# A list scheduler's prices refitted, instruction chunks counted, and ranks moved by pseudo-random offsets, in one layer of RWKV-7, gated DeltaNet and SwiGLU

## The chip, the cores and the metric

The kernel runs on one core of a Trainium2 chip, in one launch. The metric is the device time of an execution in microseconds (us), as the median of several runs. Engines are named as in the profile: PE is TensorE (matmuls), DVE is VectorE, ACT is ScalarE, POOL is GpSimd, and SP is SyncE, whose queue issues most DMA transfers.

## The reference, cut to what matters

One layer over 256 latent and 256 context tokens of 2048 channels, in fp32. The modulated, normalised input goes through one wide projection. Its columns feed two token mixers, each run in both directions: an RWKV-7 scan of 16 heads of 64 channels, and a gated DeltaNet of 8 heads of 128 channels in chunks of 64 tokens. A chunk needs the solution of a unit lower triangular system, and the chunks of a head are tied together by a state:

```python
sol = lax.linalg.triangular_solve(lmat, rhs, left_side=True, lower=True, unit_diagonal=True)
...
def step(s, inp):
    qk_i, u_i, w_i, qd_i, kt_i, gl_i = inp
    v_new = u_i - jnp.einsum('bhck,bhkv->bhcv', w_i, s)
    o = jnp.einsum('bhck,bhkv->bhcv', qd_i, s) + jnp.einsum('bhcj,bhjv->bhcv', qk_i, v_new)
    s = s * gl_i[..., None, None] + jnp.einsum('bhck,bhcv->bhkv', kt_i, v_new)
    return s, o
...
m = jax.nn.sigmoid(g_a) * (o_a @ p_a) + jax.nn.sigmoid(g_b) * (o_b @ p_b)
return m @ w_out
...
return (jax.nn.silu(gate) * up) @ w_down
```

The mixers' outputs are projected, merged with sigmoid gates and projected once more; then the layer's feed-forward part follows. The silu, sigmoid, exponential, logarithm and tanh in it run on ACT, which holds one set of function tables at a time; an instruction ACT_TABLE_LOAD brings another set.

## The kernel before, in words

**Products.** Each large fp32 product is made of three products of a shorter format. A 128x128 block of weights is split into an upper half (tile whi, a cast on ACT) and a lower half (wlo, the difference, on DVE); the activations are split likewise (hxh and hxl for the latent tokens, hch and hcl for the context, ob for the DeltaNet's output). PE then adds whi times upper, whi times lower and wlo times upper in PSUM (tile mm), each as a row "mm" of 128x256. These rows are nine tenths of PE's work; they need only the weights, so they fit anywhere. The mixers' products are small, in full fp32, and pass through the PSUM tiles s, pa and pi: 128x128 for the scans of the DeltaNet heads (tiles St for the state, Rg, Qe, Vn, aw for the parts of a step), 32x32 blocks with 16 or 32 columns for the triangular inverses (tiles iv, LT, Qm, extra, Tx). An fp32 product of this kind counts once in the listing of the program's order, and as two passes in the trace. Between two small products of a head stands work of DVE or ACT nearly always.

**Stages.** The prologue (L495 to L595: the first modulation vectors and the low-rank columns) ends at 124.5 us. From there to 1337.7 us runs what I call the weave: input projection, both mixers, and most of the projections behind them. The last stage (rest of the merge, output projection, feed-forward; products L436 to L438, casts L426 and L427) follows to the end in a fixed order.

**The scheduler.** The order within the weave is chosen while the program is built, by the class Weave (from L218). Every task is a generator that yields operations, waits for names (`yield "asked", i, q`), or asks for a buffer. `Weave.add` takes one with a rank: the products of weights have rank 900, a pair p of RWKV heads has ranks about 10p, DeltaNet head h has 100 + 10h + i. `Weave.run` (L274) holds a model of the time at which each engine is free, and picks the piece that could start first; on equal starts the lower rank. A chosen operation is appended to its engine's instructions, and the engine's modelled time grows by its price: `Lane.product` (L119) for matmuls, `Lane.cost` for the others. `Weave.turn` adds for a change of PE's tile size (into a small one, back to full, across between two small ones), with the values of `LAT` at L31. Since all operations are issued by the lambda at L164, nearly every instruction of the weave has that line in the profile; a table load that a task asks for by itself has L154.

The chip executes each engine's instructions in just this order, and semaphores hold an engine where its operand isn't there. A price that differs from the chip changes no result, only the order.

**What is told of readiness.** Two names are given out by tasks when the last of several pieces of work is done. `lowrank_out` (four per RWKV pair, j from 0 to 3) tells "lowrank" when j is 3, and `gate_out` (40 in all) tells "gates" when j is 39.

Of the kernel before, what the change touches and what calls it, by code (L numbers as in the profile page):

```python
# [2 lines left out]

# [9 lines left out]
F32R = mybir.dt.float32r  # L13
# [5 lines left out]
P = 128  # L19
# [8 lines left out]
NHELD, NB = 6, 10  # L28
GATES_A, GATES_B = ((36,0,0,0,0,0,0,0),(0,0,0,0,0,4,0,0))

LAT = dict(dma=3.1, v=1.0, s=1.0, hop=dict(e=0.215, v=0.135, s=0.15, g=0.1), slack=0.1, own=0.09, grp=32, crank=-1, cg=4, into=0.14, back=0.2, cross=0.14, stay=0.0, gpace=1.6)  # L31
LNEXP = "natural_log_exp_and_others"
SIGM = "sigmoid_and_others"
UNIT = 64 * 64 + 64
# [71 lines left out]
class Op:  # L106


    def __init__(self, lane, cost, call, mode=None, base=None):
        self.lane, self.cost, self.call, self.mode, self.base = lane, cost, call, mode, base  # L110


class Lane:
# [5 lines left out]
    def product(self, out, a):  # L119
        n, rows, m = int(np.prod(out.shape[1:])), a[0].shape[0], int(np.prod(a[0].shape[1:]))  # L120
        if a[0].dtype == F32R and n == T:
            return 0.1145, "full"
        if a[0].dtype == F32R:
            return 0.0065 + 0.000443 * n, "full"
        if rows >= 96 and m == P:
            return max(0.219, 0.012 + n * 4 / 2400), "full"
        mode = (rows, m)
        if rows < 64:
            return 0.0165, mode
        if rows == 64:  # L130
            return (0.064 if n > 64 else 0.048) if m < P else 0.02 + n * 4 / 2400, mode
        return (0.06 if m < 64 else 0.058), mode

    def cost(self, name, out, a, k):
        n = int(np.prod(out.shape[1:]))
# [14 lines left out]
    def __getattr__(self, name):  # L150

        def op(out, *a, **k):
            if name == "preload_act_table_set":
                return Op(self, 1.2, lambda: self.engine.preload_act_table_set(out))  # L154
            if name == "dma_start":
                return Op(self, 0.6 if self.each > 0.002 else 0.06, lambda: self.engine.dma_start(out, *a))
            mode = base = None
            if name == "transpose" and len(a) == 2:
                cost, mode = 0.109, "full"
            elif name == "matmul":  # L160
                cost, mode = self.product(out, a)
            else:
                cost, base = self.cost(name, out, a, k), (out.offset // out.ap[0][0], out.shape[0])
            return Op(self, cost, lambda: getattr(self.engine, name)(out, *a, **k), mode, base)  # L164
        return op


# [50 lines left out]
class Weave:  # L218


    def __init__(self):
        self.work, self.free, self.done, self.now, self.mode, self.cur, self.idle = [], {}, {}, 0.0, "full", None, True

    def add(self, rank, gen, at=None):
        now, cur = self.now, self.cur
        w = Piece(rank, gen, now if at is None else at)
        self.work.append(w)
        self.step(w, None)
        self.now, self.cur = now, cur
# [37 lines left out]

    def release(self, banks):
        banks.free.append(self.cur.shown())

    def turn(self, mode):
        return 0.0 if mode == self.mode else LAT["back"] if mode == "full" else LAT["into"] if self.mode == "full" else LAT["cross"]

    def run(self):  # L274
        while self.work:
            for w in list(self.work):
                if w.want is not None and not isinstance(w.want, (list, float)) and self.there(w):
                    self.step(w, self.take(w))
            best = None
            for w in self.work:  # L280
                if isinstance(w.want, float):
                    key = (w.seen, w.rank)
                    if best is None or key < best[0]:
                        best = (key, w, None)
                elif isinstance(w.want, list):
                    lane = w.want[0].lane
                    start = max(self.free.get(lane, 0.0), w.at(lane))
                    if lane is self.tensor and self.mode != "full" and w.want[0].mode == "full":
                        start += LAT["stay"]
                    key = (start, w.rank)  # L290
                    if best is None or key < best[0]:
                        best = (key, w, lane)
            if best is None:
                if any(w.want is not None and not isinstance(w.want, (list, float)) and self.there(w) for w in self.work):
                    continue
                assert not self.work, [w.want for w in self.work]
                return
            w, lane = best[1:]
            if lane is None:
                w.want = None  # L300
                assert w.seen < 1e5, [x.want for x in self.work]
                self.step(w, None)
                continue
            start = max(self.free.get(lane, 0.0), w.at(lane))
            ops, rest = w.want, None
            cost = 0.0
            if lane is self.tensor:
                ops, rest = ops[:LAT['grp']], ops[LAT['grp']:]
                if self.mode == "full" and ops[0].mode == "full" and start > self.free.get(lane, 0.0) + 0.02:
                    cost += 0.1  # L310
            w.want = rest or None
            got = []
            for o in ops:
                if lane is self.tensor:
                    cost += self.turn(o.mode)
                    self.mode = o.mode
                elif o.base is not None:
                    if lane.base not in (None, o.base):
                        cost += 0.08
                    lane.base = o.base  # L320
                got.append(o.call())
                cost += o.cost
            w.end = self.free[lane] = start + cost
            w.lane = lane
            if not rest:
                self.step(w, got[-1])


def emit(ctx: ExitStack, tc, A, out, dbg=None):
# [473 lines left out]
    pr[0]["kps"], pr[0]["rps"] = low[4], low[5]  # L803
    sgd = rs.tile([P, T], F32, tag="sgd", name="sgd")[:64]

    def lowrank_out(p, j, ps, so):
        yield s.activation(so, ps, AF.Sigmoid, bias=p_("w0" if j < 2 else "a0", 8 * (j % 2) + p))
        weave.release(psb)
        yield s.dma_start(sgd_[p, :, j], so)
        yield 2.5  # L810
        if j == 3:
            weave.ready("lowrank", p)

    landed = {}
# [328 lines left out]


    gts_ = dpool.tile([40, P, T], F32, name="gts_")
    gate_next = iter(range(40))

    def gate_out(pool, j, ps):
        g = pool.tile([P, T], F32, tag="gt", name="gt")
        yield s.copy(g, ps[:, :T])  # L1150
        weave.release(mmb)
        Q.dma_start(gts_[j], g)
        if j == 39:
            weave.ready("gates")

    def fetch(parts, i):
# [234 lines left out]
    class Shared:  # L1391


        def __init__(self):
            self.arena, self.iv = Places(None, arena, *gplaces), []
# [476 lines left out]
    with tc.manual_schedule(engines={mybir.EngineType.PE, mybir.EngineType.DVE, mybir.EngineType.Activation,  # L1872
                                     mybir.EngineType.SP}):
        for j in range(NB, KT):
            ps = pst(pmm, "mm")
            block(ps[:, 0:T], (j - NB) * NGH // CG, range(NGH), OB)
            m = x1p.tile([P, T], F32, tag="m", name="m")
# [15 lines left out]
        for j in range(KT):  # L1893
# [7 lines left out]
            k, a = divmod(j, 4)  # L1901
# [190 lines left out]
```

## Time and profile before

| what | value |
|---|---|
| median of 3 runs | 2196.24 us (2191.26 to 2198.05) |
| span of the profiled execution | 2188.6 us |
| prologue | 0 to 124.5 us |
| weave | 124.5 to 1337.7 us |
| last stage | 1337.7 to 2188.6 us |
| PE, DVE, ACT busy | 96%, 71%, 51% |

The profiled execution is one execution, 7.6 us under the median of the runs. In the rows, "out<-in" names the tiles that an instruction writes and reads; a bracket at the end of a row of the timeline is the engine's idle time just before it with what ended that. "issue" there means that the engine waited for nothing that the profile shows. The granted PE clock is 1 at full speed.

### The profile page before, as it was taken

Reading aid. Unit: us, or ns where it says so; the run is one execution under the profiler, and the core shown is the slowest. Engines: PE = TensorE matmul, PEld = TensorE weight load, DVE = VectorE, ACT = ScalarE, POOL = GpSimd, SP = SyncE. Lnnn points to the kernel's source line nnn. Section 1 sums busy time; section 2 is a strip of 40 time slices with the busy share of each in tenths; the row PEclk is TensorE's granted clock in tenths of the full one; section 3 lists DMA queues with packets and bytes.
Section 4 is the critical chain, followed back from the end, with each engine's and each line's share of the span. In section 5 each row is a group of like instructions: output and inputs, shape, how many; then the busy total and the mean of one; then the engine's idle time right before and its main releaser. Section 6 shows DMA issues by size and latency. Waiting matters only on the chain.

```text
span 2188.6 us, 59116 instructions
## 1 busy us (share of the span) xinstructions
PE 2108.6 (96%) x24536; PEld 1977.7 (90%) x24536; DVE 1552.5 (71%) x3308; ACT 1118.2 (51%) x2209; POOL 19.2 (1%) x55
## 2 busy tenths in 40 slices
PE   7999999999999999999999998999999999999997
PEld 5897698889888888998989987999999999999997
DVE  4466589889889976899998776865666665555554
ACT  3246654565455556565565754644444444444443
POOL 0000000000000000000000000000000000000000
PEclk9999999999999999999999999999999999999999
DMA  9966756645555554665653754856777776666665
GB/s 377 415 175 196 228 154 179 178 144 156 154 167 143 166 164 135 188 194 171 176 152 112 216 153 157 297 177 201 238 248 235 242 241 217 194 191 194 195 194 163
DMA packets 276286, 431.14 MB, mean 197 GB/s; under 512 B 119857, under 2 KB 136625, under 8 KB 271665
## 3 DMA queue, kind: packets, MB, share of 16 engines
q1 hardware_dynamic: 262192, 402.19, 59.5%
q10 hardware_dynamic: 13824, 25.17, 3.6%
q8 instruction: 192, 3.15, 0.6%
q14 instruction: 78, 0.63, 0.1%
HBM read 401.50 MB, written 25.77 MB: 195 GB/s over the span
## 4 chain that ended last, share of the span: by engine, by line
PE 80%; DVE 7%; DMA 7%; ACT 3%; issue 2%; SPq 0%; DVEq 0%; ACTq 0%
PE mm L164 26%; PE mm L438 12%; PE mm L436 12%; PE mm L437 12%; PE s L164 6%; PE pa L164 5%; PE pi L164 3%; DVE arena L164 2%; DMA wraw<-w 2%; DVE wlo L164 2%; DMA wraw<-ada_rest 1%; PE mm L529 1%; PE s L579 1%; ACT arena L164 1%; PE mm L579 1%
## 5 line engine op out<-in xcount | busy, mean ns | idle before, releaser
L427 DVE TENSOR_TENSOR wlo<-wraw,whi 128x1024 fp32r<-128x1024 f32 (+1 forms) x264 | 314.9, 1193 | 291.0 <-ACT whi L426 291.0
L426 ACT CAST whi<-wraw 128x1024 fp32r<-128x1024 f32 (+1 forms) x264 | 270.6, 1025 | 386.1 <-PE mm L437 359.5
L164 PE MATMUL mm<-hxh,wlo 128*128 128x256 f32 x1376 | 399.9, 291 | 9.5 <-DVE wlo L164 7.7
L164 PE MATMUL mm<-hxh,whi 128*128 128x256 f32 x1376 | 397.0, 288 | 2.3 <-ACT whi L164 1.3
L164 PE MATMUL mm<-hxl,whi 128*128 128x256 f32 x1376 | 395.4, 287 | 0.0
L438 PE MATMUL mm<-hfh,wlo 128*128 128x256 f32 x1344 | 371.8, 277 | 0.2 <-DVE wlo L427 0.2
L436 PE MATMUL mm<-hfh,whi 128*128 128x256 f32 x1344 | 371.2, 276 | 0.0
L437 PE MATMUL mm<-hfl,whi 128*128 128x256 f32 x1344 | 371.2, 276 | 0.0
L164 ACT CAST whi<-wraw 128x512 fp32r<-128x512 f32 (+1 forms) x398 | 242.8, 616 | 214.9 <-PE mm L164 93.2
L164 DVE TENSOR_TENSOR wlo<-wraw,whi 128x512 fp32r<-128x512 f32 (+1 forms) x398 | 270.3, 682 | 86.2 <-ACT whi L164 79.8
L164 PEld LDWEIGHTS mm<-hxh,wlo 128*128 128x128 f32 x1376 | 260.7, 189 | 19.6 <-DVE wlo L164 11.3
L164 PEld LDWEIGHTS mm<-hxh,whi 128*128 128x128 f32 x1376 | 260.6, 189 | 10.3 <-issue 4.3
L164 PEld LDWEIGHTS mm<-hxl,whi 128*128 128x128 f32 x1376 | 260.8, 190 | 6.3 <-issue 3.9
L438 PEld LDWEIGHTS mm<-hfh,wlo 128*128 128x128 f32 x1344 | 252.4, 188 | 1.2 <-DVE wlo L427 0.8
L437 PEld LDWEIGHTS mm<-hfl,whi 128*128 128x128 f32 x1344 | 252.5, 188 | 0.0
L436 PEld LDWEIGHTS mm<-hfh,whi 128*128 128x128 f32 x1344 | 252.4, 188 | 0.0
L164 PE MATMUL mm<-hch,wlo 128*128 128x256 f32 x496 | 142.5, 287 | 0.0
L164 PE MATMUL mm<-hcl,whi 128*128 128x256 f32 x496 | 142.2, 287 | 0.0
L436 PE MATMUL mm<-za,whi 128*128 128x256 f32 x512 | 141.5, 276 | 0.0
L164 PE MATMUL mm<-hch,whi 128*128 128x256 f32 x496 | 141.3, 285 | 0.2 <-issue 0.2
L438 PE MATMUL mm<-za,wlo 128*128 128x256 f32 x512 | 141.3, 276 | 0.0
L437 PE MATMUL mm<-za,whi 128*128 128x256 f32 x512 | 141.3, 276 | 0.0
(407 smaller groups left out, 4534.2 us busy)
## 6 DMA issues: line engine op xcount, KB each, us to landing
wraw<-w SPq DMA_DIRECT2D x344, 256.0 KB, 3.3
wraw<-wgu SPq DMA_DIRECT2D x168, 512.0 KB, 4.7
aw<-ada_first SPq DMA_DIRECT2D x32, 1024.0 KB, 12.2
wraw<-wdn SPq DMA_DIRECT2D x64, 448.0 KB, 3.7
wraw<-ada_rest SPq DMA_DIRECT2D x96, 256.0 KB, 3.2
aw<-ada_rest SPq DMA_DIRECT2D x48, 512.0 KB, 4.4
wraw<-wout SPq DMA_DIRECT2D x64, 256.0 KB, 5.7
aw<-ada_gt ACTq DMA_DIRECT2D x64, 256.0 KB, 5.0
```

Of the source, the lines that this page charges most:

```text
L164: return Op(self, cost, lambda: getattr(self.engine, name)(out, *a, **k), mode, base)
L426: S.copy(hi[:, c, :M], raw[:, c, :M])
L427: V.tensor_sub(lo[:, c, :M], raw[:, c, :M], hi[:, c, :M].bitcast(F32))
L436: E.matmul(ps, hi, Xh[:, k, :n], start=first and i == 0, stop=False)
L437: E.matmul(ps, hi, Xl[:, k, :n], start=False, stop=False)
L438: E.matmul(ps, lo, Xh[:, k, :n], start=False, stop=last and i == len(wt) - 1)
L529: E.matmul(ps[32 * g:32 * g + 32, 0:P], ckr[:, k].rearrange("p a b -> p (a b)"), aws[e, c][:, i, g], start=k == 0, stop=k == KT - 1)
L579: E.matmul(ps[:m, T * a:T * a + T], w_, X[:, 2 * e + k, :], start=e == k == i == 0, stop=e == NE - 1 and k == 1 and i == len(todo) - 1)
```

## The change

Six things are changed, all in the code that chooses the order, none in an operation.

- `LAT` gets new values: into 0.14 to 0.1, back 0.2 to 0.22, cross 0.14 to 0.115; two are new, fetch 3.6 and land 2.3.
- `Lane.product` prices small products anew: blocks of under 64 rows 0.0175 for 0.0165, 64-row blocks by the place of the output and the operand, 128-row ones 0.066 for 0.058.
- Every `Op` carries a number of instructions, 4 for a matmul in full fp32 and 2 otherwise.
- `Weave.fetched` counts PE's instructions in chunks of 256. Chunk c is asked for once 200 instructions of the one before are out, at least 3.6 us after the last asking, and lands 2.3 us later; PE's modelled time is held until then.
- `Weave.add` moves the rank of each piece that is added from outside the loop and has a rank below 800 by up to 8 either way, from a pseudo-random sequence with a seed (`NUDGE`, seed 202).
- The two names are told when four outputs of a pair, or 40 gates, have been counted, in whatever order they came.

```diff
+import random
-LAT = dict(dma=3.1, v=1.0, s=1.0, hop=dict(e=0.215, v=0.135, s=0.15, g=0.1), slack=0.1, own=0.09, grp=32, crank=-1, cg=4, into=0.14, back=0.2, cross=0.14, stay=0.0, gpace=1.6)
+LAT = dict(dma=3.1, v=1.0, s=1.0, hop=dict(e=0.215, v=0.135, s=0.15, g=0.1), slack=0.1, own=0.09, grp=32, crank=-1, cg=4, into=0.1, back=0.22, cross=0.115, stay=0.0, gpace=1.6, fetch=3.6, land=2.3)
+NUDGE = (202, 8.0)
...
         mode = (rows, m)
         if rows < 64:
-            return 0.0165, mode
+            return 0.0175, mode
+        if rows == 64 and m < P:
+            cross = (out.offset // out.ap[0][0]) // 64 != (a[0].offset // a[0].ap[0][0]) // 64
+            return ((0.108 if len(out.shape) > 2 else 0.057) if n > 64 else 0.032 if n < 64 else 0.0 if cross else 0.065), mode
         if rows == 64:
-            return (0.064 if n > 64 else 0.048) if m < P else 0.02 + n * 4 / 2400, mode
-        return (0.06 if m < 64 else 0.058), mode
+            return 0.02 + n * 4 / 2400, mode
+        return (0.06 if m < 64 else 0.066), mode
...
                 cost, mode = self.product(out, a)
+                insts = 2 if a[0].dtype == F32R else 4
...
+        self.inst, self.chunk, self.asked, self.lands = 0, 0, -9.0, [-9.0, -9.0]
+        self.draw = random.Random(NUDGE[0])
 
     def add(self, rank, gen, at=None):
         now, cur = self.now, self.cur
+        if cur is None and rank < 800:
+            rank += NUDGE[1] * (2 * self.draw.random() - 1)
...
+    def fetched(self, t, n):
+
+        self.inst += n
+        while self.inst > 256 * self.chunk + 200:
+            self.asked = max(t, self.asked + LAT["fetch"])
+            self.lands.append(self.asked + LAT["land"])
+            self.chunk += 1
+        return max(t, self.lands[(self.inst - 1) // 256])
...
                 if lane is self.tensor:
                     cost += self.turn(o.mode)
+                    cost = self.fetched(start + cost, o.insts) - start
                     self.mode = o.mode
...
-        if j == 3:
+        out_lows.append(p)
+        if out_lows.count(p) == 4:
             weave.ready("lowrank", p)
...
-        if j == 39:
+        out_gates.append(j)
+        if len(out_gates) == 40:
             weave.ready("gates")
```

Added lines push the helper's line from L164 to L170, and that of the separate table loads from L154 to L159. The engines' instructions are the same ones in another order, with one exception: ACT has 40 table loads where it had 34. Three places follow.

At the end of the weave PE runs the scan of the last DeltaNet head. The listing of before has, on PE, the rows from a step's first product on the state (St) to the head's output (CR), and then the next product of weights, which needs that output (ob):

```order
L164 MATMUL s<-St,arena 128x128 x2
L164 MATMUL s<-Rg,TF_12684 128x128 x2
L164 MATMUL s<-Qe,St 128x128
L164 MATMUL s<-aw,Vn 128x128
L164 MATMUL s<-Qe,St 128x128
L164 MATMUL s<-aw,Vn 128x128
L164 MATMUL s<-arena,CR 128x256
L164 MATMUL mm<-ob_18143,whi 128x256 x2
```

After, PE has products of weights between the same two steps:

```order
L170 MATMUL mm<-ob_18210,whi 128x256
L170 MATMUL s<-St,arena 128x128 x2
L170 MATMUL mm<-ob_18210,whi 128x256
L170 MATMUL mm<-ob_18210,wlo 128x256
L170 MATMUL mm<-ob_18210,whi 128x256 x2
L170 MATMUL mm<-ob_18210,wlo 128x256
L170 MATMUL mm<-ob_18210,whi 128x256 x2
L170 MATMUL mm<-ob_18210,wlo 128x256
L170 MATMUL mm<-ob_18210,whi 128x256 x2
L170 MATMUL mm<-ob_18210,wlo 128x256
L170 MATMUL s<-Rg,TF_12761 128x128 x2
```

Eleven products have moved in between, of the output projection's weights with the heads that are done already.

The second place is PE at the scan of an earlier head. Before, at 1028 us, the rows stand so, up to the next product of weights (pa with one name is a transpose):

```order
L164 MATMUL s<-St,arena 128x128 x2
L164 MATMUL pa<-arena 128x128 x4
L164 MATMUL s<-Rg,TF_12684 128x128 x2
L164 MATMUL s<-Qe,St 128x128
L164 MATMUL s<-aw,Vn 128x128
L164 MATMUL s<-Qe,St 128x128
L164 MATMUL s<-aw,Vn 128x128
L164 MATMUL pa<-C,arena 128x128 x4
L164 MATMUL pi<-iv,LT 32x16 x32
L164 MATMUL s<-arena,CR 128x256
L164 MATMUL pa<-C,arena 128x128 x4
L164 MATMUL mm<-hxh,whi 128x256
```

After, at head 6, these rows of PE follow on the four products of the scan, again up to the next product of weights:

```order
L170 MATMUL s<-aw,Vn 128x128
L170 MATMUL pa<-arena 128x128 x4
L170 MATMUL pa<-C,arena 128x128 x4
L170 MATMUL pi<-extra,LT 32x16 x32
L170 MATMUL s<-arena,CR 128x256
L170 MATMUL pa<-C,arena 128x128 x4
L170 MATMUL pi<-Qm,iv 32x16 x32
L170 MATMUL pi<-extra,LT 32x32 x16
L170 MATMUL pa<-arena,CR 128x512
L170 MATMUL pi<-iv,Qm 32x32 x16
L170 MATMUL mm<-hxh,whi 128x256
```

The rows of a scan, of a head's features and of an inverse have moved together, 16 in all with those ahead of the piece, and no product of weights stands between them.

The third place is ACT around the silu of the same head. Before, ACT has (arena names many tiles; the ACTIVATE of 128x768 is part of the head's features):

```order
L164 ACTIVATE arena<-s,C 128x256
L164 ACTIVATE arena<-arena 128x256
L164 ACT_TABLE_LOAD
L164 ACTIVATE arena<-arena 128x512
L164 CAST whi<-wraw 128x512
L164 COPY extra<-pi 32x4x16 x4
L164 ACTIVATE arena<-arena 128x768
L154 ACT_TABLE_LOAD
L164 CAST whi<-wraw 128x512
```

After, ACT has:

```order
L170 ACTIVATE arena<-arena 128x256
L170 COPY gvt<-pa 128x512
L170 ACT_TABLE_LOAD
L170 ACTIVATE arena<-arena 128x512
L170 ACT_TABLE_LOAD
L170 ACTIVATE arena<-s,C 128x256
L170 ACT_TABLE_LOAD
L170 ACTIVATE arena<-arena 128x768
L170 ACT_TABLE_LOAD
L170 ACTIVATE arena<-arena 128x256
L159 ACT_TABLE_LOAD
L170 COPY extra<-pi 32x4x16 x4
```

The ACTIVATEs of two kinds now alternate, so the tables are changed five times where they were changed twice, and the copies into extra stand behind all of them.

More of the change, by code (lines that the diff above doesn't have):

```diff
@@ L106, with __init__ @@
 class Op:
-    def __init__(self, lane, cost, call, mode=None, base=None):
-        self.lane, self.cost, self.call, self.mode, self.base = lane, cost, call, mode, base
+    def __init__(self, lane, cost, call, mode=None, base=None, insts=2):
+        self.lane, self.cost, self.call, self.mode, self.base, self.insts = lane, cost, call, mode, base, insts
 class Lane:
@@ L156, in op @@
                 return Op(self, 0.6 if self.each > 0.002 else 0.06, lambda: self.engine.dma_start(out, *a))
-            mode = base = None
+            mode, base, insts = None, None, 2
             if name == "transpose" and len(a) == 2:
@@ L161, in op @@
                 cost, mode = self.product(out, a)
+                insts = 2 if a[0].dtype == F32R else 4
             else:
                 cost, base = self.cost(name, out, a, k), (out.offset // out.ap[0][0], out.shape[0])
-            return Op(self, cost, lambda: getattr(self.engine, name)(out, *a, **k), mode, base)
+            return Op(self, cost, lambda: getattr(self.engine, name)(out, *a, **k), mode, base, insts)
         return op
@@ L221, in __init__ @@
     def __init__(self):
-        self.work, self.free, self.done, self.now, self.mode, self.cur, self.idle = [], {}, {}, 0.0, "full", None, True
+        self.work, self.free, self.done, self.now, self.mode, self.cur = [], {}, {}, 0.0, "full", None
+        self.inst, self.chunk, self.asked, self.lands = 0, 0, -9.0, [-9.0, -9.0]
+        self.draw = random.Random(NUDGE[0])
     def add(self, rank, gen, at=None):
         now, cur = self.now, self.cur
+        if cur is None and rank < 800:
+            rank += NUDGE[1] * (2 * self.draw.random() - 1)
         w = Piece(rank, gen, now if at is None else at)
@@ L804, in emit @@
     sgd = rs.tile([P, T], F32, tag="sgd", name="sgd")[:64]
+    out_lows = []
     def lowrank_out(p, j, ps, so):
@@ L1145, in emit @@
     gts_ = dpool.tile([40, P, T], F32, name="gts_")
-    gate_next = iter(range(40))
+    gate_next, out_gates = iter(range(40)), []
     def gate_out(pool, j, ps):
```

## The prediction

> **What bounds the kernel now.** First the page's head and busy times:
>
> ```profile
> span 2188.6 us, 59116 instructions
> PE 2108.6 (96%) x24536; PEld 1977.7 (90%) x24536; DVE 1552.5 (71%) x3308; ACT 1118.2 (51%) x2209; POOL 19.2 (1%) x55
> ```
>
> The profiled execution's span is 2188.6 us, 7.6 below the median of 2196.24. The sum below is a difference and is taken off the median. TensorE (PE) is busy for 96% of the span, and the change removes no matmul, so the room is PE's idle time and the time in which its clock is low. The windows by stage show where these lie (the row below gives us, then busy us and count of PE, PEld, DVE, ACT and POOL, then granted PE clock, DMA share and GB/s):
>
> ```profile
> 124.50:253.20 128.70, 120.92 (x875) 96.34 (x876) 79.57 (x174) 80.31 (x151) 2.41 (x7) 0.97 0.66 202
> 253.20:780.00 526.80, 511.15 (x8238) 465.65 (x8237) 460.00 (x1075) 286.47 (x739) 14.50 (x41) 0.99 0.57 160
> 780.00:1337.70 557.70, 535.24 (x6637) 497.22 (x6636) 455.23 (x1208) 327.50 (x728) 1.90 (x2) 0.98 0.56 165
> 1337.70:2188.60 850.90, 833.85 (x7266) 828.13 (x7265) 504.47 (x707) 388.10 (x526) 0.00 (x0) 0.99 0.68 213
> ```
>
> The weave, which the scheduler orders, is 124.5 to 1337.7; PE is idle there for 7.8 + 15.7 + 22.5 = 46 us. The stage behind it stays as it is. So even a perfect order gains at most these 46 us and what the clock loses beside them. The waits of PE within the weave, 24 rows with 69 waits and 45.7 us in all, say what it waits for; these are the first two and the last:
>
> ```profile
> PE mm L164 <- DVE wlo L164: 7.7, 15, 1.5
> PE pi L164 <- issue: 5.1, 5, 2.1
> ...
> PE pi L164 <- ACT iv L164: 0.2, 1, 0.2
> ```
>
> No row dominates. What matters is what PE has to do between a step of a head and the next: a product row (mm, 128x256) needs only cast weights and fills a wait; where the order gives a long row of small matmuls (s, pa, pi) without a product, every wait shows. I call nine or more such rows a bare stretch. Before has three; their windows, the last one followed by what comes right behind it:
>
> ```profile
> 1028.40:1039.40 11.00, 7.82 (x99) 6.32 (x98) 11.00 (x29) 8.06 (x15) 0.00 (x0) 0.75 0.61 177
> 1125.20:1145.40 20.20, 16.40 (x244) 13.59 (x247) 19.93 (x50) 13.23 (x29) 0.00 (x0) 0.83 0.57 161
> 1311.10:1321.10 10.00, 5.30 (x36) 4.17 (x34) 5.02 (x14) 2.76 (x7) 0.00 (x0) 0.97 0.78 275
> 1321.10:1328.00 6.90, 6.87 (x33) 6.70 (x34) 4.78 (x9) 1.45 (x3) 0.00 (x0) 0.54 0.23 91
> ```
>
> Length less PE busy is idle: 3.2, 3.8 and 4.7, together 11.7 us. The clock column falls to 0.75, 0.83 and, behind the last, 0.54, where the stages above have 0.97 to 0.99. Taking one minus clock over each window as lost work gives 2.75 + 3.4 + 0.3 + 3.2 = 9.6 us (a little too much, since an idle PE loses nothing to a clock). The three cost 21.3 us.
>
> **Bare stretches.** The order after has two: one of 9 rows with 5 waits on other engines, and one of 16 rows with 14 waits, at head 6. The three of before held 9, 11 and 10. The last head's scan, bare before, now has 10 to 15 products between its steps. What the long stretch of after will take is built from the tail of before, where the same scan step stands bare, and from what ScalarE (ACT) does:
>
> ```profile
> 429.13 1.24 PE L164 MATMUL pi<-arena,Tx 32*32 32x16 f32 x100 [1.30 <-issue]
> ...
> 1027.12 0.28 PE L164 MATMUL mm<-hxh,whi 128*128 128x256 f32 x1
> 1027.24 0.28 PE L164 MATMUL mm<-hxl,whi 128*128 128x256 f32 x1
> 1027.35 0.38 PE L164 MATMUL s<-Qe,St 128*128 128x128 f32 x2
> 1027.57 0.39 PE L164 MATMUL s<-aw,Vn 128*128 128x128 f32 x2
> ...
> 1033.43 0.49 PE L164 MATMUL s<-aw,Vn 128*128 128x128 f32 x2 [1.45 <-DVE Vn L164]
> ```
>
> ```profile
> 1313.63 0.68 PE L164 MATMUL s<-St,arena 128*128 128x128 f32 x4
> ...
> 1318.00 0.70 PE L164 MATMUL s<-arena,CR 128*128 128x256 f32 x2 [1.10 <-ACT arena L164]
> 1321.13 0.58 PE L164 MATMUL mm<-ob,whi 128*128 128x256 f32 x1 [2.43 <-ACT ob L164]
> ```
>
> ```profile
> 1128.00 1.28 ACT L164 ACT_TABLE_LOAD   x1
> 1129.30 0.63 ACT L164 ACTIVATE arena<-arena 128x512 f32<-128x512 f32 x1
> 1132.97 0.84 ACT L164 ACTIVATE arena<-arena 128x768 f32<-128x768 f32 x1 [3.04 <-DVE arena L164]
> 1133.83 1.28 ACT L154 ACT_TABLE_LOAD   x1
> 1135.12 0.27 ACT L164 COPY arena<-s 128x128 f32<-128x128 f32 x1
> ...
> 1140.69 0.85 ACT L164 COPY iv<-pi 32x64 f32<-32x64 f32 x4
> ...
> 1317.53 0.42 ACT L164 ACTIVATE arena<-arena 128x256 f32<-128x256 f32 x1 [3.27 <-DVE arena L164]
> 1318.74 0.47 ACT L164 ACTIVATE arena<-s,C 128x256 f32<-128x256 f32 x1 [0.79 <-PE s L164]
> ```
>
> ```profile
> L164 ACT COPY gvt<-pa 128x512 f32<-128x512 f32 x5 | 2.9, 577 | 0.1
> ```
>
> From the first product on St to the end of the Square on ACT is 1313.63 to 1317.95, 4.3 us. Then after queues on ACT, ahead of the copies extra<-pi on which PE's next burst waits: gvt 0.58, five table loads of 1.28 (6.4), and four ACTIVATEs, 0.63 + 0.47 + 0.84 + 0.42; together 9.3. The copies take 0.85, and one DVE step (1.2, the longest wait on one in the pi bursts) may lie between: 15.7 us in all. PE's own work in them is 16 products and six transposes of two passes at 0.11 (two passes from 1027.35 to 1027.57), 4.8, the wider product at 0.45, and 64 products of 32 rows, 128 passes, at 1.24 per hundred (row 429.13), 1.6: 6.9. So 8.8 are lost, and at the 0.20 of clock per us that the first two stretches lose on average (6.2 over 31.2), 3.1 more: 11.9.
>
> In the last head's scan 11 products at 0.12 (1027.12 to 1027.24) cover 1.3 us, more than the 1.10 of row 1318.00. The final wait, 2.43 in row 1321.13, remains, as nothing follows that scan: 2.4, and half of the clock that was lost behind it, 1.6: 4.0. So after loses 15.9 where before lost 21.3, **−5.4**. The stretch with 5 waits at 0.36 each (3.2 over 9 in before's first) gives **+1.8**.
>
> For the clock I weigh a rule. In window 1028.40 to 1039.40 the clock is 0.75 with no idle longer than 1.45 us (row 1033.43). The Trainium skill ("TensorE: Matmul & The Clock Gate", "HAM oscillation — how this bites in real kernels") asks only that there be no idle gaps of PE above about 3.4 us. By that rule the clock would not follow these stretches at all, and the time is that of the fourth rival; the trace disagrees so far.
>
> **Table loads.** ACT gets six more in all, 34 to 40:
>
> ```profile
> L154 ACT ACT_TABLE_LOAD x15 | 19.2, 1283 | 0.3
> ```
>
> Six at 1.28 are 7.7 us of an engine that is busy 51%. Three of them are the head-6 ones just counted; the other three lie at places with products on PE and cost 0 there; were that cover gone, 3.8.
>
> **The start of the weave.** Before, the load falls into an idle time of ACT; after, it stands behind k<-mm and ahead of the next cast:
>
> ```profile
> 128.87 1.28 ACT L154 ACT_TABLE_LOAD   x1
> 134.85 0.69 ACT L164 ACTIVATE k<-mm,om 128x512 f32<-128x512 f32 x1 [4.71 <-PE mm L579]
> 135.44 0.61 ACT L164 CAST whi<-wraw 128x512 fp32r<-128x512 f32 x1
> ...
> 137.30 0.39 PE L164 MATMUL mm<-hxh,wlo 128*128 128x256 f32 x1 [0.19 <-DVE wlo L164]
> ```
>
> The cast comes 1.28 later, and behind it in ACT's queue stand the next casts; PE already waits 0.19 for the part that follows from such a cast. Bounds 0 and 1.3, taken 0.7 since PE has some products in hand: **+0.7**.
>
> **Instruction chunks.** The waits "issue" fall inside the bursts of 32-row products, which use up instructions fastest; the longest:
>
> ```profile
> 814.03 0.25 PE L164 MATMUL pi<-arena,Tx 32*32 32x16 f32 x7 [2.08 <-issue]
> ```
>
> Between the first two long bursts of each of the eight RWKV pairs, before has 1 to 18 products, 84 in all, and after 11 to 30, 118 in all. The pair at 814 has 8 and waits 2.08, but that at 429 (row above) has 12 and waits 1.30, so spacing alone doesn't decide. I take half of the longest: **−1.0**, bounds −5.1 (all five waits) and 0.
>
> **All else.** Refitted prices and rank offsets move some thousand rows; the counts of waits and of mode switches hardly change (547 to 543). The rest of PE's waits, 45.7 − 11.7 − 5.1 = 29, is drawn anew: 0, bounds ±5 (a sixth of it). SP's and POOL's instructions are as many as before, and DMA engines are busy for 0.56 to 0.66 in the weave, so loads cost 0.
>
> Sum: −5.4 + 1.8 + 0.7 − 1.0 = −3.9, so 2196.24 − 3.9 = **2192.3 us**, 0.2% less. About 0.3%, 6.6 us, is what a measurement of this kernel tells from no change: faster is below 2189.6, slower above 2202.8.
>
> **Rivals.** *One, faster: the 14 waits cost what the old ones did.* The five loads don't wait for data; they may run while ACT would wait anyway (row 1132.97: 3.04 idle). Then each wait costs 0.39 (11.7 over 30), 5.5 in all, with no clock lost, and the tail 2.4: 7.9 for 21.3, −13.4. With the fetch wait of 2.08 gone, −13.4 + 1.8 + 0.7 − 2.1 = −13.0, **2183**. For it: idle ACT times ahead of all such ACTIVATEs. Against: five loads in a row with a copy behind them that PE needs. It decides once 2.7 us of the sum fall away.
>
> *Two, slower: casts come late.* The lower half of each weight, wlo, is made by DVE between the heads' steps:
>
> ```profile
> L164 DVE TENSOR_TENSOR wlo<-wraw,whi 128x512 fp32r<-128x512 f32 (+1 forms) x398 | 270.3, 682 | 86.2 <-ACT whi L164 79.8 <-DMA tscr<-arena 3.1 <-PE pa L164 0.5
> ```
>
> 15 of the 398 now hold PE up, 7.7 us, 0.51 each. DVE is busy for 460.0 of 526.8 us in 253 to 780. If the new ranks put one more DVE step ahead of the casts and one in ten of the 383 that hold nothing up came late by as much, 38 more waits make +19.4; −3.9 + 19.4 = +15.5, **2211.7**. It decides at (6.6 + 3.9) / 0.51, 21 more waits. Against: DVE changes its partition base less often (934 for 967).
>
> *Three: each load drains ACT.* If a load also stopped what is behind it for 1.4 us more, the five would give 7.0 more: **2199**. Against: the op behind the load at 1133.83 starts at 1135.12, with no gap. This drain is the Trainium skill's ("ScalarE: Activation LUTs", "What ACT_TABLE_LOAD costs"): about 1380 ns on top of 1283.
>
> *Four: the clock doesn't follow the stretches.* Then 11.7 go and 8.8 + 2.4 come, −0.5 for −5.4: **2197**. Against: the clock column.
>
> That the counted chunks change nothing at all drops the −1.0: 2193, within the forecast.
>
> **How the numbers follow.** Forecast 0.43, rivals 0.40, 0.10, 0.04, 0.03 in their order. Faster is the first rival, 0.40; three and four join the forecast within 0.3%: 0.50; slower 0.10. Low end: the first rival with all fetch waits gone and nothing lost at the start, −13.4 − 5.1 + 1.8 = −16.7, 2179.5. High end: the clock lost at 0.25 per us in the long stretch (3.9 for 3.1), the start at 1.3, the rest at +5, no fetch gain: −4.6 + 1.8 + 1.3 + 5 = +3.5, 2200 in round numbers. The forecast alone would reach from 2187 to 2200.
>
> **What would show it.** In the profile after: about 16 us at head 6's scan with little PE work and five table loads in a row on ACT; the last scan with its waits filled but for the last of about 2.4; a clock of 0.8 there and near 1 at the end of the weave; a row "PE pi <- issue" of about 4. The forecast is wrong if PE's idle time in the weave changes by over 5 us elsewhere, above all in the row of waits for wlo, or if the five loads lie in ACT's idle time.

## The result, and the profile after

The changed kernel takes 2208.7 us (median, 2204.5 to 2216.2), before 2194.7 beside it: ratio 1.0075, interval 1.0050 to 1.0099. It is slower by about 14 us, where 2192.3 was forecast and 2200 was the upper end. The head of the page after:

```profile
span 2202.7 us, 59130 instructions
PE 2107.4 (96%) x24536; PEld 1974.8 (90%) x24536; DVE 1554.0 (71%) x3308; ACT 1126.3 (51%) x2215; POOL 21.3 (1%) x55
```

The weave now ends at 1349.6. The same windows of both kernels, first after (whole weave, its start, a part of the RWKV stage, the rest), then before (columns as in the prediction):

```profile
126.50:1349.60 1223.10, 1167.21 (x15742) 1058.17 (x15743) 996.81 (x2455) 701.96 (x1621) 20.89 (x50) 0.98 0.57 166
126.50:400.00 273.50, 255.37 (x2943) 219.51 (x2944) 198.86 (x435) 152.55 (x319) 6.93 (x19) 0.99 0.59 176
400.00:780.00 380.00, 373.51 (x6120) 339.29 (x6120) 342.24 (x810) 212.90 (x554) 12.05 (x29) 1.00 0.60 166
780.00:1349.60 569.60, 538.34 (x6684) 499.37 (x6683) 455.71 (x1212) 336.51 (x748) 1.90 (x2) 0.96 0.54 161
```

```profile
124.50:1337.40 1212.90, 1167.01 (x15742) 1058.91 (x15743) 994.49 (x2454) 694.18 (x1615) 18.82 (x50) 0.98 0.57 167
124.50:400.00 275.50, 264.18 (x3108) 228.19 (x3109) 205.62 (x451) 158.94 (x341) 6.85 (x19) 0.99 0.62 184
400.00:780.00 380.00, 367.89 (x6005) 333.80 (x6004) 333.95 (x799) 207.85 (x548) 10.07 (x29) 0.99 0.56 157
780.00:1337.40 557.40, 534.94 (x6634) 496.92 (x6633) 454.93 (x1207) 327.40 (x727) 1.90 (x2) 0.98 0.56 165
```

PE is busy in the weave for 1167.2 us after and 1167.0 before; nearly all of the 10.2 us by which the weave is longer is idle time (55.9 for 45.9). (The rows mm take 862 of these 1167 us before, so within the weave they are three quarters of PE's work and not nine tenths.) Up to 400 us the new order is worse: idle 18.1 for 11.3. From 400 to 780 it is better: idle 6.5 for 12.1. Behind that it is worse again: idle 31.3 for 22.5, and the clock is at 0.96 for 0.98. The remaining 3.9 us of the span lie ahead of the weave and behind it, in code that is the same; the start of the weave alone moves between 122 and 127 us from one profile to another, so nothing is read from them. The longest rows of PE's waits in the weave after:

```profile
PE pi L170 <- ACT extra L170: 6.7, 1, 6.7
PE pa L170 <- ACT kkn L170: 5.6, 3, 3.3
PE pi L170 <- DVE arena L170: 5.5, 8, 1.3
PE pi L170 <- DVE iv L170: 4.9, 1, 4.9
PE s L170 <- ACT lo L170: 4.8, 7, 1.2
PE mm L170 <- DVE wlo L170: 3.5, 11, 0.9
PE pi L170 <- DMA extra<-tscr: 2.9, 2, 2.6
```

Before, no single wait was over 2.43, the final one. Here four are: 6.7 for the copies into extra, 4.9 for iv, 3.3 for kkn (at 267 us, in the start of the weave), 2.6 for a transfer into extra.

The first is the long bare stretch (at the sixth DeltaNet head's features, counted from one). PE's rows in the middle of it, and ACT's:

```profile
1090.27 0.62 PE L170 MATMUL pi<-extra,LT 32*32 32x16 f32 x32 [1.94 <-DVE extra L170]
...
1100.61 0.65 PE L170 MATMUL pi<-extra,LT 32*32 32x32 f32 x32 [6.74 <-ACT extra L170]
```

```profile
1089.89 0.42 ACT L170 ACTIVATE arena<-arena 128x256 f32<-128x256 f32 x1 [5.00 <-DVE arena L170]
1090.22 0.57 ACT L170 COPY gvt<-pa 128x512 f32<-128x512 f32 x1
1090.80 1.28 ACT L170 ACT_TABLE_LOAD   x1
1092.10 0.63 ACT L170 ACTIVATE arena<-arena 128x512 f32<-128x512 f32 x1
1092.74 1.28 ACT L170 ACT_TABLE_LOAD   x1
...
1098.41 1.28 ACT L159 ACT_TABLE_LOAD   x1
1099.71 0.85 ACT L170 COPY extra<-pi 32x64 f32<-32x64 f32 x4
```

ACT runs with no gap over 0.03 us from 1089.89 to 1100.56, five loads among it, and PE stands. The windows of the stretch, of what comes behind it, of the 17 us at half clock, and of the last head's scan:

```profile
1082.10:1104.60 22.50, 11.82 (x235) 8.59 (x234) 16.84 (x42) 14.72 (x24) 0.00 (x0) 0.68 0.50 154
1104.60:1107.60 3.00, 3.00 (x20) 3.00 (x16) 2.77 (x6) 2.92 (x10) 0.00 (x0) 0.57 0.72 198
...
1323.30:1334.40 11.10, 8.67 (x74) 8.19 (x72) 6.05 (x15) 5.12 (x12) 0.00 (x0) 1.00 0.79 293
1334.40:1340.00 5.60, 5.48 (x31) 5.29 (x32) 4.29 (x9) 1.24 (x2) 0.00 (x0) 0.70 0.51 181
```

```profile
1082.10:1090.10 8.00, 4.99 (x66) 4.18 (x65) 7.46 (x20) 2.74 (x6) 0.00 (x0) 1.00 0.75 225
1090.10:1093.80 3.70, 3.54 (x102) 2.85 (x102) 3.68 (x10) 3.65 (x5) 0.00 (x0) 0.50 0.74 268
...
1090.10:1107.10 17.00, 9.34 (x180) 6.91 (x180) 11.68 (x28) 14.40 (x27) 0.00 (x0) 0.50 0.42 129
```

The stretch idles 10.7 us. The half clock begins at 1090.1, as PE comes back from the wait of 1.94, and not with the wait of 6.74, which begins at 1093.87. The last scan idles 2.4, only its final wait, with the clock at 1.00.

The wait for iv is of another kind: it isn't in a bare stretch. Products stand right ahead of the two bursts and right behind them. PE's rows about it, and DVE's queue:

```profile
987.52 0.28 PE L170 MATMUL mm<-hxh,wlo 128*128 128x256 f32 x1
987.73 0.51 PE L170 MATMUL pi<-iv,LT 32*32 32x16 f32 x32
993.12 0.63 PE L170 MATMUL pi<-iv,LT 32*32 32x16 f32 x32 [4.88 <-DVE iv L170]
993.68 0.58 PE L170 MATMUL mm<-hxh,whi 128*128 128x256 f32 x1
```

```profile
988.09 0.34 DVE L170 SCALAR_TENSOR_TENSOR LT<-pa,nbtok,arena 128x128 f32<-128x128 f32 x1
988.35 1.27 DVE L170 SCALAR_TENSOR_TENSOR aw<-aw,ck 128x1024 f32<-128x1024 f32 x1
989.54 0.41 DVE L170 TENSOR_TENSOR aw<-pa,arena 128x256 f32<-128x256 f32 x1
989.88 0.47 DVE L170 SCALAR_TENSOR_TENSOR arena<-mm,PR,arena 128x254 f32<-128x254 f32 x1
990.26 0.41 DVE L170 TENSOR_TENSOR aw<-pa,arena 128x256 f32<-128x256 f32 x1
990.60 0.47 DVE L170 SCALAR_TENSOR_TENSOR arena<-mm,PR,arena 128x255 f32<-128x255 f32 x1
990.99 0.43 DVE L170 STREAM_TRANSPOSE iv<-LT 64x256 f32<-64x256 f32 x1
```

As the rows stand, the transposes that PE waits for could follow on the last LT at 988.43; five instructions of other work stand ahead of them, 2.6 us of the 4.88.

### The profile page after: what moved, and what is told of

Read it like the earlier page. It is cut to its first block, busy times and chain, and to the rows that moved or that the text cites. A ratio compares the mean times of both kernels' runs of the same rounds, so it can differ in the third digit from the quotient of the medians.

```text
span 2202.7 us, 59130 instructions
## 1 busy us (share of the span) xinstructions
PE 2107.4 (96%) x24536; PEld 1974.8 (90%) x24536; DVE 1554.0 (71%) x3308; ACT 1126.3 (51%) x2215; POOL 21.3 (1%) x55
## 4 chain that ended last, share of the span: by engine, by line
PE 73%; DVE 6%; DMA 5%; ACT 3%; issue 1%; SPq 0%; ACTq 0%; DVEq 0%
PE mm L170 24%; PE mm L458 12%; PE mm L457 12%; PE mm L456 12%; PE s L170 6%; PE pa L170 5%; PE pi L170 2%; DMA wraw<-w 2%; DVE arena L170 1%; DVE wlo L170 1%; DMA wraw<-wgu 1%; DMA wraw<-ada_rest 1%; ACT whi L170 1%; ACT arena L170 1%; DVE wlo L447 0%
## 5 line engine op out<-in xcount | busy, mean ns | idle before, releaser
L170 PE MATMUL mm<-hxh,wlo 128*128 128x256 f32 x1376 | 396.5, 288 | 3.9 <-DVE wlo L170 3.5
L170 PE MATMUL mm<-hxh,whi 128*128 128x256 f32 x1376 | 397.3, 289 | 2.6 <-ACT whi L170 1.9
L170 PE MATMUL mm<-hxl,whi 128*128 128x256 f32 x1376 | 393.5, 286 | 0.0
L170 ACT CAST whi<-wraw 128x512 fp32r<-128x512 f32 (+1 forms) x398 | 244.0, 616 | 204.0 <-PE mm L170 122.9
L170 DVE TENSOR_TENSOR wlo<-wraw,whi 128x512 fp32r<-128x512 f32 (+1 forms) x398 | 270.6, 681 | 86.1 <-ACT whi L170 83.4
L170 PEld LDWEIGHTS mm<-hxh,wlo 128*128 128x128 f32 x1376 | 260.2, 189 | 13.3 <-DVE wlo L170 6.4
L170 PEld LDWEIGHTS mm<-hxh,whi 128*128 128x128 f32 x1376 | 260.1, 189 | 11.4 <-issue 3.9
L170 PEld LDWEIGHTS mm<-hxl,whi 128*128 128x128 f32 x1376 | 260.5, 189 | 7.2 <-issue 4.1
L170 PE MATMUL mm<-hch,wlo 128*128 128x256 f32 x496 | 143.4, 289 | 0.0
L170 PE MATMUL mm<-hcl,whi 128*128 128x256 f32 x496 | 143.3, 289 | 0.0
L170 PE MATMUL mm<-hch,whi 128*128 128x256 f32 x496 | 142.7, 288 | 0.0
```

## The experiments

All ratios are to the kernel before on the same chip, five rounds, with a 95% interval.

### The table loads

**One head's silus as copies.** In `features`:

```diff
-        yield s.activation(k, k, AF.Silu)
-        yield s.activation(vq, vq, AF.Silu)
+        f = AF.Identity if h == 5 else AF.Silu
+        yield s.activation(k, k, f)
+        yield s.activation(vq, vq, f)
```

> The changed kernel with the two silus of one DeltaNet head's features, those in the long bare stretch, replaced by a plain copy through the same engine (the head's features are then not silu'd): order and instructions as in the changed kernel, less four of the five table loads that stand in a row there. Theory A (the loads are in the chain that PE waits for, and the idle PE then gets half its clock): the wait of 6.74 us for the copies into extra falls by 4 x 1.28 = 5.1 to about 1.6, the half clock of 17.07 us behind it to about 10, so the time falls by 7 to 9 us against the changed kernel, to a ratio to before of about 1.003. Theory B (the loss is spread over many small waits and the loads run beside other waits): the time stays within 2 us of the changed kernel, ratio 1.006 to 1.008.

Measured: 2206.6 us, ratio 1.0061 (1.0040 to 1.0081). The place itself does as theory A says; PE's row, and the windows from the stretch's start to its end and of the half clock:

```profile
1097.12 0.65 PE L170 MATMUL pi<-extra,LT 32*32 32x32 f32 x32 [1.95 <-ACT extra L170]
```

```profile
1083.50:1101.60 18.10, 11.69 (x234) 8.46 (x233) 16.75 (x42) 9.23 (x20) 0.00 (x0) 0.73 0.66 195
...
1091.80:1105.40 13.60, 10.37 (x185) 7.93 (x180) 12.29 (x28) 9.31 (x23) 0.00 (x0) 0.50 0.58 167
```

The wait is 1.95 for 6.74, the stretch 18.1 for 22.5, the half clock 13.6 for 17. But the whole gains about 3 us, 1.0061 for 1.0075, and the two intervals are each some 5 us wide to either side, so neither no gain nor the 7 to 9 of theory A can be excluded. The loads are in the chain there; nothing shows that they are the 14 us.

**All silus of the weave as copies, in both kernels.** The same at all heads and at the output gate, and the explicit table load behind each left out.

> The changed kernel with all nine silus of the weave (eight heads' features and the gate of the heads' outputs) as plain copies and without the explicit table loads behind them (the silus are left out of what is computed): 18 table loads in place of 40, same order. Theory A: 7 to 9 us as in the run with one head's silus, and little more, since other loads stand beside products: ratio to before 1.002 to 1.004. Rival: table loads cost wherever they stand, about half of 1.28 each: 22 x 0.64 = 14 us, ratio 1.000 to 1.001. Theory B: within 2 us of the changed kernel.

> The kernel before with the same nine silus as plain copies and without the explicit loads behind them (left out of what is computed): 16 table loads in place of 34, same order. Theory A (a load costs only where PE waits behind it): 0 to 3 us less than before. Rival (a load costs about half of 1.28 wherever it stands): 18 x 0.64 = 11.5 us less, ratio 0.995.

Measured: 1.0032 (1.0013 to 1.0051) after, 0.9985 (0.9972 to 0.9997) before. That is 0.43% or 9.4 us off the changed kernel and 3.3 off the one before: the loads, with the switching between silu and exponentials, explain some 6 of the 14 us, with an uncertainty as large. With the loads out of both, the changed order is still slower by 0.47%, 10 us. In the order of before, a load costs 0.2 us on average (3.3 over 18), not 0.64.

**The first silu issued right ahead of the second**, with what is computed kept:

```diff
+        first, second = s.activation(k, k, AF.Silu), s.activation(vq, vq, AF.Silu)
+        calls = first.call, second.call
+        first.call, second.call = (lambda: None), (lambda: [c() for c in calls])
+        yield first
+        yield second
```

> The changed kernel with the first silu of each head's features issued right ahead of the second, at the place where the second stood; the scheduler's times are as they were, so every other instruction stays where it is. In the long bare stretch three table loads stand where five did. Theory A: the wait of 6.74 us for the copies into extra falls by 2 x 1.28 = 2.6, and the half clock of 17.07 us may be one step of 3.4 shorter: 2.6 to 4.3 us less than the changed kernel, ratio 1.0055 to 1.0063. Theory B (loads hidden): no change, ratio 1.007 to 1.008.

Measured: 1.0070 (1.0052 to 1.0088), no gain that can be told. Two loads are gone, but the wait fell by 1.44 only: with the loads out of its way ACT now stands 1.29 for PE.

```profile
1103.68 0.65 PE L170 MATMUL pi<-extra,LT 32*32 32x32 f32 x32 [5.30 <-ACT extra L170]
```

```profile
1096.59 0.47 ACT L170 ACTIVATE arena<-s,C 128x256 f32<-128x256 f32 x1 [1.29 <-PE s L170]
```

### The parts of the change

**No offsets** (`NUDGE = (202, 0.0)`):

> The changed kernel with offsets of zero (NUDGE amplitude 0): new prices and counted chunks, ranks as before. Its order has bare stretches of 11, 9 and 13 rows and 40 table loads, none of them five in a row. Theory A (this draw's order is the trouble, not the prices): near before, ratio 0.998 to 1.003. Rival (the new prices or the counted chunks make the order worse): as slow as the changed kernel, ratio 1.005 to 1.010.

Measured: 1.0164 (1.0140 to 1.0189), 36 us. Theory A falls with this: new prices without the offsets are worse than with them. With offsets of zero the counting of chunks never delays anything, and PE's order is the same without it; so this is the prices alone. The new way of telling the two names changes nothing either: with it or without it, the kernel before, the changed kernel and this one have the same instructions in the same order on every engine.

**The offsets alone, and the two halves of the prices alone**, each put into the kernel before: the lines of `add` with `NUDGE = (202, 8.0)`; into, back and cross; `product`.

> The kernel before with the offsets alone (seed 202, amplitude 8; old prices, no counted chunks, readiness as before). 40 table loads, bare stretches of 13 and 14 rows. Theory C (the new prices make orders worse, and the offsets win part of that back): about as before, ratio 0.997 to 1.003. Theory D (the order of before is a good draw, and whatever redraws it costs, prices or offsets alike): ratio 1.004 to 1.015.

> The kernel before with the new values of into, back and cross alone (offsets none, product prices old). 42 table loads, one bare stretch of 10 rows. With zero offsets the new prices together cost 36 us. Theory C: this part or the other (the product prices) carries them, ratio over 1.010 in one of the two and 0.997 to 1.003 in the other. Theory D: both redraw the order, both 1.004 to 1.015. By bare stretches alone this one would be faster than before, ratio about 0.995.

> The kernel before with the new prices of small products alone (offsets none, into, back and cross old). 36 table loads, no bare stretch of nine rows. Theory C: over 1.010 or 0.997 to 1.003, the other way from the run with into, back and cross alone. Theory D: 1.004 to 1.015. By bare stretches alone it would be 15 to 20 us faster than before, ratio 0.991 to 0.993.

Measured: 1.0082 (1.0062 to 1.0101), 1.0180 (1.0159 to 1.0202) and 1.0160 (1.0142 to 1.0179). Each alone is as slow as the changed kernel or slower, and the two halves of the prices don't add up to the whole (1.0164). Orders with one bare stretch or none are among the slowest: bare stretches don't rank orders.

**The chunks not counted**, in the changed kernel:

```diff
-        return max(t, self.lands[(self.inst - 1) // 256])
+        return t
```

> The changed kernel with the chunk counting out of force (Weave.fetched returns the time unchanged). In the changed kernel the counting delays PE's modelled time just once, by 5 ns, at instruction 12034; without it the order differs in 1597 rows of PE behind that place, with bare stretches of 20 and 10 rows and 36 table loads. Theory D (a redraw moves the time by some us whatever causes it): 5 us or more off the changed kernel, either way. Theory C: within 3 us of it, ratio 1.006 to 1.009, since 5 ns say nothing of the chip. If the rows of the issue waits grow by 3 us or more, the counting does what its name says.

Measured: 1.0161 (1.0135 to 1.0186). Leaving out a delay of 5 ns in the model, once, costs 0.86%, 19 us. The issue waits do grow, as the expectation's last sentence has it; first the changed kernel, then this one:

```profile
PE pi L170 <- issue: 1.5, 3, 0.9
PE mm L170 <- issue: 0.3, 1, 0.3
```

```profile
PE pi L170 <- issue: 4.3, 6, 2.1
PE mm L170 <- issue: 3.1, 2, 1.7
```

They make 5.6 of the 19. Since 5 ns at one place can't say where the chip waits for instructions hundreds of rows on, this is no proof that the counting works; the rest is other waits.

### Other draws

**Seed 1**, with old prices and with new ones:

> The kernel before with offsets from seed 1 in place of none (old prices, no counting): another draw of the order. 38 table loads, bare stretches of 17 and 10 rows. Theory D: slower than before like every other redraw so far, by 15 to 40 us, ratio 1.007 to 1.018. Rival (a draw is as often faster as slower than before): ratio below 1.003.

> The changed kernel with seed 1 in place of 202: another draw with the new prices. 34 table loads, one bare stretch of 19 rows. Theory D, with 202 as one of the better draws: 2210 to 2232, ratio 1.008 to 1.018. Rival (seed 202 is an unlucky draw of good prices): near or below before, ratio under 1.003.

Measured: 1.0115 (1.0089 to 1.0141) and 1.0110 (1.0089 to 1.0131). The prices make no difference that can be told between these two. Nor do they with seed 202: 1.0082 with old prices (the offsets alone, above), 1.0075 with new ones (the changed kernel). Only without offsets do old and new prices differ, 1 for 1.0164.

**A part of the changed order kept.** At a given time of the scheduler the ranks of the waiting pieces are set anew, with or without the old prices (only the turn itself is shown; the first two runs also go back to the old prices there):

```diff
+            if not self.turned and self.free.get(self.tensor, 0.0) > LATE[0]:
+                self.turned = True
+                for w in self.work:
+                    w.rank = w.late
```

> The changed kernel up to the scheduler's time 660 (PE's row 4662), from there the old prices and ranks without offsets. PE's order is the changed kernel's before that row and a fresh draw behind it, with no bare stretch of nine rows; 36 table loads. Theory E (the loss of the changed kernel lies in the part from 900 us on, in the places at 988, 1084 to 1104 and 1245 us; its part from 400 to 780 us is better than that of before): 10 to 18 us less than the changed kernel, 2187 to 2197 where before is 2190, ratio 0.997 to 1.003. Rival F (any order drawn anew loses 15 to 40 us, wherever): no better than the changed kernel, ratio 1.006 or more.

> The same with the turn at the scheduler's time 760 (PE's row 5187), old prices and ranks without offsets behind it; 37 table loads, no bare stretch. Theory E: ratio 0.997 to 1.003, the sum of idle time and half of the half-clocked time from 900 us on 31 to 38 us instead of 51. Rival F: ratio 1.006 or more.

> The changed kernel up to the scheduler's time 660, from there the offsets of seed 1 for those of seed 202, the new prices kept; PE's order differs from row 5201 on; 36 table loads, no bare stretch. Theory E: ratio 0.997 to 1.003, as with the old prices behind the turn, since the draw decides and not the prices. If the new prices are what costs: above 1.006 here, and below 1.003 in the two runs with old prices behind the turn.

> The changed kernel up to the scheduler's time 760, from there the offsets of seed 2, new prices kept; PE's order differs from row 5917 on; 37 table loads, no bare stretch. This order still has the place at 988 us as it was, while the long bare stretch with its five table loads is gone. Theory E: 5 to 10 us less than the changed kernel, ratio 1.002 to 1.005, and the wait of 4.88 us at 988 is still there.

Measured: 1.0102 (1.0071 to 1.0133), 1.0103 (1.0080 to 1.0125), 1.0063 (1.0042 to 1.0085), 1.0081 (1.0055 to 1.0107). Theory E falls: with the bad places gone from the order, new ones come (in the fourth the wait for iv is still there, 4.96, as expected), and none of the four is faster than the changed kernel beyond its interval. From 780 to 1360 us PE idles 29.8 to 36.4 us in the four, 31.5 in the changed kernel and 23.8 before. Nor was the part ahead of that better than before: from 135 to 780 us PE idles 23.8 to 25.6 in the four, 24.6 in the changed kernel and 23.4 before, since the changed order loses up to 400 us what it gains behind. In the second run idle time and half of the half-clocked time come to about 41 us from 900 us on (27.5 idle, and 0.03 of 452 us), where 31 to 38 was expected. Old prices behind the turn aren't better than new ones.

### One price by 0.1 ns, and by 1 ns

The kernel before with one number changed: the price of a VectorE instruction 0.0701 for 0.07; of a weight product 0.1146 for 0.1145; of a ScalarE instruction 0.061 for 0.06.

> The kernel before with one number changed that cannot matter by itself: the scheduler's fixed price of a VectorE instruction 0.0701 for 0.07 us, 0.1 ns. PE's order is the same up to about row 4227 and differs behind it (972 rows); 38 table loads, one bare stretch of 15 rows. Theory D (the order of before is a good draw; whatever redraws it costs 15 to 40 us, a redraw of only the last part less): slower than before by 5 to 20 us, ratio 1.002 to 1.009. Theory C (the offsets and prices cost by what they say): same as before, ratio 0.998 to 1.002. In either case the time of the weave should be 1142 us, plus PE's idle time, plus half of the time at half clock, as it was within 4 us in the kernels run so far.

> The kernel before with the scheduler's price of a weight product 0.1146 for 0.1145 us, 0.1 ns; nothing else. PE's order differs from row 1013 on, in 2079 rows, about as many as with the new prices (2196 and 2229 with either half of them). 41 table loads, one bare stretch of nine rows. Theory F (the order of before is a good draw, and any that is drawn anew from the first part of the weave loses 15 to 40 us): ratio 1.007 to 1.018. Theory C (the content of the new prices and offsets is what costs): no change, ratio 0.998 to 1.002.

> The kernel before with the scheduler's fixed price of a ScalarE instruction 0.061 for 0.060 us, 1 ns; nothing else. PE's order differs from row 1081 on, in 1679 rows. 34 table loads, one bare stretch of 13 rows. Theory F: ratio 1.005 to 1.018, a little less than with 0.1 ns on the products since fewer rows differ. Theory C: ratio 0.998 to 1.002.

Measured: 1.0010 (0.9995 to 1.0024), 1.0138 (1.0117 to 1.0158) and 1.0040 (1.0025 to 1.0055). A tenth of a nanosecond on one price costs 29 us when it redraws the order from the first part of the weave; 1 ns on another costs 9; a redraw from row 4227 on costs nothing that can be told, less than theory D said. The weave of the 2221 us kernel, and of the one that is as fast as before:

```profile
126.10:1367.30 1241.20, 1174.15 (x15743) 1064.11 (x15744) 994.09 (x2455) 705.64 (x1623) 19.36 (x50) 0.98 0.55 163
```

```profile
122.20:1334.90 1212.70, 1167.89 (x15743) 1058.23 (x15744) 992.56 (x2455) 699.28 (x1619) 18.83 (x50) 0.98 0.56 167
```

Idle 67.0 us in the first and 44.8 in the second, before 45.9. The 0.1 ns kernel's waits are spread like this, many kinds and none alone:

```profile
PE pi L164 <- issue: 10.6, 7, 3.6
PE pa L164 <- ACT arena L164: 7.6, 5, 3.8
PE pi L164 <- DVE Qm L164: 5.8, 5, 1.7
```

The expectation that a weave is 1142 us plus idle plus half of the half-clocked time missed by 5 in the kernel that is as fast as before (1207 for 1212.7), so it is only a rough account.

## Why the prediction was wrong, point by point

- **The long bare stretch: the mechanism was right, the size was too small.** Forecast: 15.7 us up to PE's burst behind the copies, 8.8 lost and 3.1 of clock. Measured from 1082.16 to 1100.61: 18.4, idle 10.7 over the stretch, and one minus clock gives 0.32 x 22.5 + 0.43 x 3 = 8.5. The 4.3 from the first product on St to the end of the Square became 8.15 (1082.16 to 1090.31), as ACT stood 5.00 for DVE; the DVE step of 1.2 didn't come. The clock is mis-sized by 5 in the prediction's measure, which counts idle time too; over PE's busy time alone it is 0.32 x 11.8 + 0.43 x 3 = 5.1.
- **The tail: right.** It was to keep 2.4 of idle and 1.6 of clock; it has 2.43 and 0.30 x 5.6 = 1.7. The products between the steps cover the other waits.
- **The short stretch** was to cost 1.8. It idles 0.4, with the clock at 1.00:

```profile
1036.80:1041.30 4.50, 4.09 (x146) 3.35 (x144) 4.44 (x12) 4.32 (x13) 0.00 (x0) 1.00 0.22 37
```

- **The one table load at the start of the weave** can't be read: its own time scatters by more than the 0.7 forecast.
- **Instruction chunks.** Issue waits of pi fell from 5.1 to 1.5, by 3.6 for the 1.0 forecast, within its bounds. That the counting as such brought this isn't shown: it delayed the model once, by 5 ns, and the order so drawn has fewer such waits.
- **"All else … is drawn anew: 0, bounds ±5": this is the step that failed.** Outside the three stretches and the issue waits, before idled 45.9 − 11.7 − 5.1 = 29.1; after, outside the long stretch, the tail and the issue waits, it is 55.9 − 10.7 − 2.4 − 1.5 = 41.3 (with the 0.4 of the short stretch). That is 12 more where 0 was put, and 4.9 + 3.3 + 2.6 of the new time are three single waits that stand in no bare stretch. It is the sign of being wrong that the prediction named, though not in the row of wlo. Two mistakes are in it. A redraw was taken to be as likely to gain as to lose, but the thirteen other orders that were drawn anew, from the first part of the weave or from its middle on, all lost (five of them keep a part of the changed order, so they aren't thirteen independent draws); only the one redrawn from row 4227 on by 0.1 ns did not, as far as can be told. And waits were looked for only where PE's own rows stand bare; the wait for iv arises in DVE's queue.
- **The whole sum.** The forecast's idle terms come to −11.7 + 8.8 + 2.4 + 1.8 + 0.7 − 1.0 = +1.0 and its clock terms to −9.6 + 3.1 + 1.6 = −4.9. Measured are +10.0 of idle time, +0.2 of PE's busy time, in which a slower clock would show, and 3.9 outside the weave. So of the 18 us between forecast and result 9 are idle time, 5 are the clock's gain that didn't come, and 4 can't be read.
- **Rivals.** The first (the loads hidden) is wrong at the place: 6.74 us of idle, with ACT busy without a gap. The second gave 2211.7, near the 2208.7 measured, by luck: waits for wlo fell from 7.7 to 3.5. The third is wrong: behind the load at 1090.80 the next instruction starts at 1092.10, with no 1.4 between. That no drain shows here is against the sentence of the Trainium skill ("ScalarE: Activation LUTs", "What ACT_TABLE_LOAD costs") that it went with. The fourth is wrong too: the clock is 0.50 for 17 us about that stretch. Its rule, of the Trainium skill ("TensorE: Matmul & The Clock Gate", "HAM oscillation — how this bites in real kernels"), isn't saved by the 6.74 us, as the clock falls 3.8 us before that wait begins. Nor is it in the kernel with one head's silus as copies, where the clock is 0.50 for 13.6 us about the same place and the longest idle is 1.95.

**What is shown and what isn't.** Shown: the changed kernel idles in places that its order makes; its prices alone and its offsets alone cost as much or more; and so do 0.1 ns that say nothing of the chip. So a new draw of the order in place of the old one is enough for a loss of this size, and nothing that the new prices, the counting or the offsets say is needed for it. Whether the new prices are nearer to the chip can't be told: with seeds 1 and 202 old and new ones give the same time within their intervals. Open: why the order of before is better than all these redraws. Its idle time says that it is, not why. An order that had once been kept as the fastest of many would look like this, whatever its prices; no run here tests that. No version here beats it; the one with silus left out computes something else.

## What to carry to other kernels

A greedy scheduler turns a price that moves by a tenth of a nanosecond into another program, 29 us slower here; the slowest draw, with new values of into, back and cross alone, was 39 us slower. So a refit of its prices is judged over several draws for each set of prices, and an order is accepted for its own measured time. Here, an order drawn anew from the first part or the middle of the weave on cost 9 to 39 us, and no change of prices won that back. When an order is read ahead of a run, look at the queues of the engines that feed the waiting one as well, and count what stands ahead of the awaited instruction, as for iv and for the five table loads.

## What the runs showed of the hardware that was not expected

Once it has fallen in a badly filled stretch, the clock stays low to the stretch's end and some us into the dense products behind it, and not in proportion to the longest wait: 17 us at 0.50 with PE busy for 9.3 of them (2.5 us into the products), and 13.6 at 0.50 with PE busy for 10.4 (3.8 us into them) when the longest wait was 1.95. What sets the length isn't shown.
